# The first and second weight sums of a feed-forward chunk kept in other tiles

## The chip, the cores and the metric

The kernel runs on one core of a Trainium2 chip (trn2). The metric is the device time of one execution in microseconds. The profile is of one such execution; its times are counted from the start of its span.

## What is computed

Four layers of a transformer trunk on 256 tokens of width 1024, all in f32. Each layer is a feed-forward stage, an attention (differential, MoBA, NSA, differential) and a second feed-forward stage, each between two norms, so there are eight feed-forward stages:

```
def swiglu(x, w_in, w_out):
    gate, up = jnp.split(x @ w_in, 2, axis=-1)
    return (jax.nn.silu(gate) * up) @ w_out
...
h = h + 0.5 * rms_norm(swiglu(rms_norm(h, g[0]), ffn_w_in[i, 0], ffn_w_out[i, 0]), g[1])
```

`w_in` is 1024 x 5632, `w_out` 2816 x 1024. The attention is not touched by the change.

## The kernel before

**Splitting.** To keep f32 accuracy every operand of a matmul is split in two: ScalarE (ACT) rounds it to `hi` (line 156), VectorE (DVE) takes the rest, `lo = x - hi` (line 157). A product is then three matmuls (hi hi, lo hi, hi lo), at line 152 for the first products and lines 244 to 246 for the output product.

**Tiles.** Weights arrive as raw tiles of 128 x 2048 f32 (1 MB). A feed-forward stage has nine raw tiles, three in a pool of the whole program and six in a pool of the stage (`homes`). A split weight is a "unit", a hi and a lo tile; there are four units (the split ring). A unit comes free when the last matmul that reads it is done.

**Chunks.** The hidden width of 2816 is worked in six chunks, 512 columns each but for chunk 1 with 256. Chunks 0 and 1 are plain. Chunks 2 to 5 (`wino`, line 475) are multiplied by Winograd's form of the 2 x 2 block product (two token tiles; two halves of the inner dimension; gate and up), with seven products in place of eight. It needs sums of the quarters of the weights, b00 and b01 (upper half, gate and up), b10 and b11 (lower half): t1 = b00 + b01, t3 = b01 + b11, t2 = t1 + b11, t4 = t2 + b10. Matching signs are in the sums of the activations (lines 270 to 273).

Two of these sums are made by DVE (`add`, line 372) and two by an accumulating DMA that POOL issues (`add_by_dma`, line 375). Before the change t1 is made in b00 in place, t3 in b01 in place, t2 in a fifth raw tile, which is claimed without a load, and t4 there by DMA.

**Order.** `loads` and `preps` are two lists of steps, and `fill` (line 407) takes steps from them: loads while fewer than nine raw tiles are live, splits while fewer than four units are live. It is called behind each product. The preps of a wino chunk j, with the output weights ("o") of chunk j-1 among them, are written by `plan_wino` (line 359) in this order: split b00; split b10, then t1 and the DMA for t3; split o; t2, split t2, then the DMA for t4; splits of t1, t3, b11; the second o; the split of t4. TensorE's products of the chunk come in the order b00, b10, t2, t1, t3, b11, t4. Between them stand the transposes of the previous chunk's result (`turn`, line 439), which need its `g` (`up`, line 431), and its output products.

The program is written out in this order, and a scheduler of the framework then sets the order on each engine ahead of time. It lets an instruction pass others when its inputs are ready by its own estimate, and it gives a raw tile to whatever first writes to it. So the order in the trace is not always that of the source. At run time every engine and every DMA queue works in its fixed order; SP issues the loads (line 312).

Of the kernel before, what the change touches and what calls it, by code (L numbers as in the profile page):

```python
# [46 lines left out]
class Trunk:  # L47
# [235 lines left out]
    def ffn(self, l, f, X, ahead, end):  # L283
        nc = self.nc
        with self.tc.tile_pool(name=f"ffn{l}{f}", bufs=2, reuse_waits="tile") as pool:
# [8 lines left out]
            loads, preps = [], []  # L294

            def raw(n, src=None):
                live["raw"] += 1
                self.n += 1
                home = homes.pop(0)
                more = {} if home is self.raw else {"bufs": RAWS - 3}  # L300
                r = home.tile([P, 2048], F32, tag="raw", name=f"raw{self.n}", **more)
                R[n] = r
                H[n] = home
                if src is not None:
                    W, r0, nk, c0, w = src
                    v = r.rearrange("p (k n) -> p k n", n=w)[:, :nk] if nk * w == 2048 else \
                        r[:, :nk * w].rearrange("p (k n) -> p k n", n=w)
                    s = W[r0:r0 + nk * P, c0:c0 + w].rearrange("(k p) n -> p k n", p=P)
                    m = 1 if self.first_units > 0 else nk
                    self.first_units -= 1  # L310
                    for k in range(0, nk, m):
                        nc.sync.dma_start(v[:, k:k + m], s[:, k:k + m])
                    shape[n] = (nk, w, min(m, nk // 2) if n[0] == 0 and n[1] != "o" else nk)
                    if self.first_units == 2:
                        self.load_x(1)
# [3 lines left out]
            def free(n):  # L319
                R.pop(n)  # L320
                homes.append(H.pop(n))
                live["raw"] -= 1

            def split(n, of, done=False):
                live["unit"] += 1
                self.n += 1
                nk, w, m = shape.get(of, (4, 512, 4))
                hi = self.wt.tile([P, nk, w], F32R, tag="hi", name=f"hi{self.n}")
                lo = self.wt.tile([P, nk, w], F32R, tag="lo", name=f"lo{self.n}")
                v = R[of][:, :nk * w].rearrange("p (k n) -> p k n", n=w)  # L330
                for k in range(0, nk, m):
                    self.hilo(v[:, k:k + m], hi[:, k:k + m], lo[:, k:k + m])
                if done:
                    free(of)
                U[n] = hi, lo, nk, w
# [23 lines left out]
            def plan_wino(j):  # L359


                c0, w = chunks[j]
                name = lambda n: (j, n)
                quarter = lambda k, u: (w_in, k * 512, 4, u * D_FF + c0, w)
                c1, w1 = chunks[j - 1]
                ko = [((j - 1, "o", k), (w_out, c1 + k * P, 2, 0, D)) for k in range(0, w1 // P, 2)]
                for n, src in ((name("b00"), quarter(0, 0)), (name("b01"), quarter(0, 1)),
                               (name("b10"), quarter(1, 0)), (name("b11"), quarter(1, 1)), (name("t2"), None), *ko):
                    loads.append(lambda n=n, src=src: raw(n, src))

                def add(to, a, b):
                    nc.vector.tensor_tensor(R[name(to)], R[name(a)], R[name(b)], op=ALU.add)  # L372

                def add_by_dma(to, b):
                    nc.gpsimd.dma_start(R[name(to)], R[name(b)], accum_op=ALU.add)  # L375

                def quarters(n, then=()):
                    split(name(n), name(n))
                    for x in then:
                        (add if len(x) == 3 else add_by_dma)(*x)  # L380

                def last_of(n, of, gone=None):
                    split(name(n), name(of), True)
                    if gone:
                        free(name(gone))

                outs = [lambda n=n: split(n, n, True) for n, _ in ko]

                def split_t2():
                    add("t2", "b00", "b11")  # L390
                    quarters("t2", [("t2", "b10")])

                preps.extend([
                    lambda: quarters("b00"),
                    lambda: quarters("b10", [("b00", "b00", "b01"), ("b01", "b11")]),
                    outs[0],
                    split_t2,
                    lambda: last_of("t1", "b00"),
                    lambda: last_of("t3", "b01"),
                    lambda: last_of("b11", "b11")])  # L400
                if j < last:
                    preps.extend(outs[1:])
                preps.append(lambda: last_of("t4", "t2", "b10"))
                if j == last:
                    preps.extend(outs[1:])

# [123 lines left out]
            for j in range(1, last + 1):  # L530
                if j in WINO:
                    plan_wino(j)
                else:
                    plan_plain(j)
                    plan_out(j - 1)
# [795 lines left out]
```

## Time and profile before

| | us |
|---|---|
| median of 3 runs | 1992.58 (1991.72 to 1995.25) |
| the profiled execution | 1992.68 |
| its span, first to last instruction | 1991.0 |
| PE busy | 1934.5 |
| DVE busy | 1610.7 |
| ACT busy | 1261.7 |

The span is the time on the chip from the first to the last instruction, 1.7 us less than the execution's own time. Busy times are sums over all stages. Matmuls are pipelined, and each one's duration is longer than the step to the next, so PE's busy time doesn't show short gaps; the timeline does.

### The profile page before, as it was taken

To read this page: it belongs to the slowest core of one execution; us is meant where nothing else is said; L and a number is where in the kernel's file an instruction comes from. 1 tells how busy PE (TensorE), PEld (TensorE's weight loads), DVE (VectorE), ACT (ScalarE), POOL (GpSimd) and SP (SyncE) were. 2 spreads that over 40 slices of the span, in tenths; PEclk is the share of its full clock that TensorE was granted. 3 is DMA by queue.
4 is the path that set the end of the run, shared out by engine and by line. 5 is a ranking of instruction groups with operands and counts; after the bars stand their busy time and mean duration, and the time that the engine had idled before them with its cause. 6 is when DMAs were issued, how large, how long until landed. Compare 5 with 4: busy or idle time off the path is not lost.

```text
span 1991.0 us, 25740 instructions
## 1 busy us (share of the span) xinstructions
PE 1934.5 (97%) x9712; PEld 1582.6 (79%) x9712; DVE 1610.7 (81%) x2040; ACT 1261.7 (63%) x1721; POOL 187.2 (9%) x303
## 2 busy tenths in 40 slices
PE   7999999999999999999999998999999999999998
PEld 6788878788878878878887887678788788878787
DVE  6799678799789766789879977877998798678797
ACT  6566666566566666566656666865666567576564
POOL 0000210000000120000000032000000000210000
PEclk9999999999999999999999999999999999999999
DMA  9795638696787556587868775166879685638692
GB/s 359 215 281 161 211 118 314 162 283 209 258 238 236 182 191 212 189 246 232 291 199 244 210 205 165 58 242 191 238 214 322 177 285 161 202 106 306 176 289 64
DMA packets 177867, 430.25 MB, mean 216 GB/s; under 512 B 8784, under 2 KB 37712, under 8 KB 169552
## 3 DMA queue, kind: packets, MB, share of 16 engines
q1 hardware_dynamic: 168528, 361.51, 50.7%
q0 software_dynamic: 9216, 67.11, 18.1%
q8 instruction: 76, 1.25, 0.3%
q14 instruction: 47, 0.39, 0.1%
HBM read 360.43 MB, written 1.05 MB: 182 GB/s over the span
## 4 chain that ended last, share of the span: by engine, by line
PE 66%; DVE 11%; issue 10%; DMA 6%; ACT 4%; POOL 0%; POOLq 0%; DVEq 0%; ACTq 0%
PE pb L152 12%; PE ps L152 8%; PE y L244 7%; PE y L246 7%; PE y L245 7%; PE pc L152 6%; DVE lo L157 5%; PE pw L675 4%; DMA raw<-raw 4%; PE pw L677 4%; PE pw L676 3%; PE pa L152 3%; ACT hi L156 2%; DMA raw<-in_ffn_w_in 2%; DVE raw L372 2%
## 5 line engine op out<-in xcount | busy, mean ns | idle before, releaser
L157 DVE TENSOR_TENSOR lo<-raw,hi 128x2048 fp32r<-128x2048 f32 (+3 forms) x534 | 981.0, 1862 | 227.1 <-ACT hi L156 226.5
L156 ACT CAST hi<-raw 128x2048 fp32r<-128x2048 f32 (+3 forms) x534 | 818.9, 1560 | 327.0 <-PE y L246 168.9
L244 PE MATMUL y<-hi,gh 128*128 128x512 f32 x704 | 278.5, 396 | 0.0
L245 PE MATMUL y<-lo,gh 128*128 128x512 f32 x704 | 274.4, 390 | 0.0
L246 PE MATMUL y<-hi,gl 128*128 128x512 f32 x704 | 267.4, 393 | 0.0
L152 PE MATMUL ps<-hi,xh 128*128 128x256 f32 (+1 forms) x512 | 175.4, 343 | 1.9 <-ACT xh L156 1.3
L152 PE MATMUL ps<-lo,xh 128*128 128x256 f32 (+1 forms) x512 | 173.1, 338 | 0.2 <-DVE lo L157 0.2
L152 PE MATMUL ps<-hi,xl 128*128 128x256 f32 (+1 forms) x512 | 172.9, 338 | 0.0
L675 PE MATMUL pw<-hi,xh 128*128 128x512 f32 (+2 forms) x432 | 164.6, 381 | 0.0
L152 PE MATMUL pb<-lo,sh 128*128 128x512 f32 x384 | 153.4, 400 | 5.7 <-DVE lo L157 5.7
L677 PE MATMUL pw<-hi,xl 128*128 128x512 f32 (+2 forms) x432 | 155.7, 360 | 0.0
L676 PE MATMUL pw<-lo,xh 128*128 128x512 f32 (+2 forms) x432 | 155.4, 360 | 0.0
L375 POOL DMA_DIRECT2D raw<-raw x64 | 55.5, 868 | 1059.7 <-DVE raw L372 506.9
L246 PEld LDWEIGHTS y<-hi,gl 128*128 128x128 f32 x704 | 131.6, 188 | 29.1 <-DVE gl L157 1.5
L152 PE MATMUL pb<-hi,sh 128*128 128x512 f32 x384 | 153.5, 400 | 0.5
L244 PEld LDWEIGHTS y<-hi,gh 128*128 128x128 f32 x704 | 132.3, 188 | 27.1 <-ACT gh L156 1.2
L245 PEld LDWEIGHTS y<-lo,gh 128*128 128x128 f32 x704 | 132.4, 188 | 26.3
L152 PE MATMUL pb<-hi,sl 128*128 128x512 f32 x384 | 150.2, 391 | 0.0
L372 DVE TENSOR_TENSOR raw<-raw,raw 128x2048 f32<-128x2048 f32 x64 | 146.3, 2286 | 0.3
L152 PEld LDWEIGHTS ps<-hi,xh 128*128 128x128 f32 x512 | 97.6, 191 | 13.1 <-ACT xh L156 2.2
L152 PEld LDWEIGHTS ps<-lo,xh 128*128 128x128 f32 x512 | 97.7, 191 | 11.2 <-DVE lo L157 1.1
L152 PEld LDWEIGHTS ps<-hi,xl 128*128 128x128 f32 x512 | 97.4, 190 | 11.1 <-DVE xl L157 1.1
(213 smaller groups left out, 3301.4 us busy)
## 6 DMA issues: line engine op xcount, KB each, us to landing
raw<-in_ffn_w_in SPq DMA_DIRECT2D x172, 1024.0 KB, 8.9
raw<-in_ffn_w_out SPq DMA_DIRECT2D x88, 1024.0 KB, 9.7
raw<-raw POOLq DMA_DIRECT2D x64, 1024.0 KB, 8.1
raw<-in_diff_w_in SPq DMA_DIRECT2D x24, 1024.0 KB, 5.3
raw<-in_moba_w_in SPq DMA_DIRECT2D x12, 1024.0 KB, 5.1
raw<-in_nsa_w_in SPq DMA_DIRECT2D x9, 1024.0 KB, 5.1
raw<-in_diff_w_out SPq DMA_DIRECT2D x8, 1024.0 KB, 4.9
gpre<-in_norm_g SPq DMA_DIRECT2D x12, 512.0 KB, 6.3
```

The source lines that it names most:

```text
L152: nc.tensor.matmul(out, l, r, start=first and i == 0, stop=last and i == len(steps) - 1, skip_group_check=more)
L156: self.nc.scalar.copy(hi, src)
L157: self.nc.vector.tensor_tensor(lo, src, hi.bitcast(F32), op=ALU.subtract)
L244: nc.tensor.matmul(y[b], x[0][:, kt, :], hi[:, k, s], start=f, stop=False)
L245: nc.tensor.matmul(y[b], x[0][:, kt, :], lo[:, k, s], start=False, stop=False)
L246: nc.tensor.matmul(y[b], x[1][:, kt, :], hi[:, k, s], start=False, stop=l)
L372: nc.vector.tensor_tensor(R[name(to)], R[name(a)], R[name(b)], op=ALU.add)
L375: nc.gpsimd.dma_start(R[name(to)], R[name(b)], accum_op=ALU.add)
L675: nc.tensor.matmul(out, x[0][:, kt, :], hi[:, k, :], start=first and i == 0, stop=False)
L676: nc.tensor.matmul(out, x[0][:, kt, :], lo[:, k, :], start=False, stop=False)
L677: nc.tensor.matmul(out, x[1][:, kt, :], hi[:, k, :], start=False, stop=last and i == len(todo) - 1)
```

## The change

t1 gets the tile that was claimed without a load, and is written right behind the split of b00 (in the source, ahead of the split of b10), with the DMA for t3 behind it. t2 is then made in b00, whose own split is done, and t4 in b00 too, by DMA. b11 is loaded third and b10 last; before, b10 was third and b11 fourth.

```
-                for n, src in ((name("b00"), quarter(0, 0)), (name("b01"), quarter(0, 1)),
-                               (name("b10"), quarter(1, 0)), (name("b11"), quarter(1, 1)), (name("t2"), None), *ko):
+                for n, src in ((name("b00"), quarter(0, 0)), (name("b01"), quarter(0, 1)), (name("t1"), None),
+                               (name("b11"), quarter(1, 1)), (name("b10"), quarter(1, 0)), *ko):
...
-                def quarters(n, then=()):
-                    split(name(n), name(n))
-                    for x in then:
-                        (add if len(x) == 3 else add_by_dma)(*x)
-
-                def last_of(n, of, gone=None):
-                    split(name(n), name(of), True)
-                    if gone:
-                        free(name(gone))
+                def first():
+                    split(name("b00"), name("b00"))
+                    add("t1", "b00", "b01")
+                    add_by_dma("b01", "b11")
+
+                def second():
+                    add("b00", "t1", "b11")
+                    split(name("t2"), name("b00"))
+                    add_by_dma("b00", "b10")
+
+                def fourth():
+                    split(name("t4"), name("b00"), True)
+                    free(name("b10"))
...
-                def split_t2():
-                    add("t2", "b00", "b11")
-                    quarters("t2", [("t2", "b10")])
-
                 preps.extend([
-                    lambda: quarters("b00"),
-                    lambda: quarters("b10", [("b00", "b00", "b01"), ("b01", "b11")]),
+                    first,
+                    lambda: split(name("b10"), name("b10")),
                     outs[0],
-                    split_t2,
-                    lambda: last_of("t1", "b00"),
-                    lambda: last_of("t3", "b01"),
-                    lambda: last_of("b11", "b11")])
+                    second,
+                    lambda: split(name("t1"), name("t1"), True),
+                    lambda: split(name("t3"), name("b01"), True),
+                    lambda: split(name("b11"), name("b11"), True)])
                 if j < last:
                     preps.extend(outs[1:])
-                preps.append(lambda: last_of("t4", "t2", "b10"))
+                preps.append(fourth)
```

## Rows read from the trace of the kernel before

**Rows 1.** The page: busy time and share of the span of each engine

```profile
PE 1934.5 (97%) x9712; PEld 1582.6 (79%) x9712; DVE 1610.7 (81%) x2040; ACT 1261.7 (63%) x1721; POOL 187.2 (9%) x303
```

**Rows 2.** Waits of PE: who waited for whom, us in total, times, longest

```profile
PE tpg L439 <- DVE g L431: 20.8, 17, 1.3
...
PE pb L152 <- DVE lo L157: 5.7, 8, 0.7
```

**Rows 3.** Timeline of PE, first stage, chunk 3: start, us, instruction, [idle before]

```profile
90.82 0.33 PE L439 MATMUL tpg<-ident,g 128*128 128x128 f32 x1 [1.25 <-DVE g L431]
...
96.48 0.33 PE L439 MATMUL tpg<-ident,g 128*128 128x128 f32 x1 [1.33 <-DVE g L431]
...
100.13 0.50 PE L152 MATMUL pb<-lo,sh 128*128 128x512 f32 x1 [0.72 <-DVE lo L157]
```

**Rows 4.** Busy time by window: PE, PEld, DVE, ACT, POOL, PE clock, DMA

```profile
80.60:97.62 17.02, 14.44 (x65) 11.09 (x64) 17.02 (x12) 9.65 (x8) 0.84 (x1) 1.00 0.82 246
```

**Rows 5.** Timeline of DVE, first stage, the same stretch

```profile
80.60 2.29 DVE L157 TENSOR_TENSOR lo<-raw,hi 128x2048 fp32r<-128x2048 f32 x1 [2.87 <-ACT hi L156]
...
97.78 4.49 DVE L157 TENSOR_TENSOR lo<-raw,hi 128x2048 fp32r<-128x2048 f32 x2 [0.16 <-ACT hi L156]
```

**Rows 6.** Timeline of ACT, first stage, chunk 2

```profile
78.67 1.91 ACT L156 CAST hi<-raw 128x2048 fp32r<-128x2048 f32 x1 [3.26 <-DMA raw<-raw]
...
85.02 1.92 ACT L156 CAST hi<-raw 128x2048 fp32r<-128x2048 f32 x1 [0.36 <-DMA raw<-in_ffn_w_out]
```

**Rows 7.** Waits of ACT for the accumulating DMA, in all

```profile
ACT hi L156 <- DMA raw<-raw: 32.3, 10, 3.5
```

**Rows 8.** Timeline of ACT: the two of these that stand in chunk 5

```profile
650.98 1.91 ACT L156 CAST hi<-raw 128x2048 fp32r<-128x2048 f32 x1 [2.33 <-DMA raw<-raw]
...
1659.18 1.91 ACT L156 CAST hi<-raw 128x2048 fp32r<-128x2048 f32 x1 [2.66 <-DMA raw<-raw]
```

**Rows 9.** Timeline of PE, first stage: last reads of two units

```profile
61.08 0.39 PE L246 MATMUL y<-hi,gl 128*128 128x512 f32 x1
...
76.76 0.39 PE L246 MATMUL y<-hi,gl 128*128 128x512 f32 x1
```

**Rows 10.** Timeline of POOL: issue of the accumulating DMA for t4, chunks 2 and 3

```profile
70.40 0.86 POOL L375 DMA_DIRECT2D raw<-raw  x1 [16.53 <-DVE lo L157]
...
100.38 0.86 POOL L375 DMA_DIRECT2D raw<-raw  x1 [9.13 <-DVE lo L157]
```

**Rows 11.** Line 375, all 64 of them

```profile
DMA to landing us min/median/max: 6.9/8.1/10.6
```

**Rows 12.** Timeline of DVE, first stage, chunk 2

```profile
60.72 2.29 DVE L157 TENSOR_TENSOR lo<-raw,hi 128x2048 fp32r<-128x2048 f32 x1 [5.84 <-ACT hi L156]
63.05 2.29 DVE L372 TENSOR_TENSOR raw<-raw,raw 128x2048 f32<-128x2048 f32 x1
...
67.81 6.69 DVE L157 TENSOR_TENSOR lo<-raw,hi 128x2048 fp32r<-128x2048 f32 x3
```

**Rows 13.** Timeline of DVE, first stage, chunk 1: the first sum of chunk 2

```profile
49.96 2.29 DVE L372 TENSOR_TENSOR raw<-raw,raw 128x2048 f32<-128x2048 f32 x1
...
52.59 2.29 DVE L157 TENSOR_TENSOR lo<-raw,hi 128x2048 fp32r<-128x2048 f32 x1
```

**Rows 14.** Timeline of SP: loads of the weights

```profile
34.39 11.49 SPq L312 DMA_DIRECT2D raw<-in_ffn_w_in  x4
...
72.32 0.37 SPq L312 DMA_DIRECT2D raw<-in_ffn_w_in  x1
74.52 4.45 SPq L312 DMA_DIRECT2D raw<-in_ffn_w_out  x2
...
108.58 0.37 SPq L312 DMA_DIRECT2D raw<-in_ffn_w_in  x1
```

**Rows 15.** Timeline of DVE, chunk 3: the split of b11

```profile
105.44 2.29 DVE L157 TENSOR_TENSOR lo<-raw,hi 128x2048 fp32r<-128x2048 f32 x1 [0.35 <-ACT hi L156]
```

**Rows 16.** Timeline of PE, chunk 3: first read of lo of b11

```profile
111.31 0.39 PE L152 MATMUL pb<-lo,sh 128*128 128x512 f32 x1
```

## The prediction

> **What bounds the kernel now.** I read the page's busy times first: PE is busy for 1934.5 of 1991.0 us, 97% [rows 1]. So there is little to gain, and only where PE stands still. The waits of PE come next. Within the feed-forward stages two causes stand out [rows 2]: the transposes (line 439) wait for `g` from DVE, 20.8 us in 17 waits, and a product waits for `lo` from DVE, 5.7 us in 8. Eight is the number of feed-forward stages. The timeline of PE shows the place, the same in each stage, in the change from chunk 2 to chunk 3: waits of 1.25, 1.33 and 0.72 us at 90.82, 96.48 and 100.13 in the first stage [rows 3], 3.30 us per stage and 26.4 us in eight.
>
> What holds PE there is DVE's queue. From 80.60 to 97.62 DVE is busy for 17.02 of 17.02 us [rows 4], and PE only waits for what stands in that queue. The stretch begins with the lo of chunk 2's t4 at 80.60, for which DVE had idled 2.87 us, waiting for ACT's hi [rows 5]. That hi began at 78.67, behind 3.26 us of idle time that ended with the accumulating DMA [rows 6]. Two things are wanted by this split. One is a free unit: the last matmul on it ends at 76.76 + 0.39 = 77.15 [rows 9]. The other is the sum t4, whose DMA POOL issued at 70.40 [rows 10] and which arrived 8.27 us later; all 64 take 6.9 to 10.6 us, median 8.1 [rows 11]. The DMA came last. ACT had been free since 78.67 - 3.26 = 75.41, so the unit alone would have held it to about 77.20, 1.79 us of the 3.26.
>
> Why was the DMA issued at 70.40? It follows the lo of t2, the first of the three at 67.81 [rows 12], which follows the sum t2 at 63.05. That sum began right where the split of "o" of chunk 1 ended (60.72 + 2.29 = 63.01), though DVE had idled 5.84 us before that split [rows 12]. I read this as a wait for a raw tile: SP's four loads from 34.39 on [rows 14] had taken what was free, and t2's tile was the one that this split gave back.
>
> **The change, part by part.** Counts and sizes don't change: two DVE sums of 2.28 us and two accumulating DMAs per wino chunk, the same loads of 1 MB. What moves is when they can start.
>
> *The second sum, t2 into b00.* It needs no new tile, only t1, b11 and the finished split of b00. In chunk 2 it can go into DVE's 5.84 us of idle time before 60.72 (2.29 fit), and cover is found for it there at no cost. That the scheduler would take it forward is my inference from the first sum of chunk 2: it runs at 49.96, ahead of the lo of b10 at 52.59, behind which it is written [rows 13]. Then hi of t2 waits for its unit only, to 61.08 + 0.39 = 61.47 [rows 9], and ends at 61.5 + 1.9 = 63.4. Its lo follows to 65.7, and POOL can issue at 65.7 instead of 70.40. With 8.27 us the sum lands at 74.0, with the longest seen, 10.6, at 76.3. Both are before 77.15, so the wait for this DMA goes and the unit is late next. Worth: 3.26 - 1.79 = 1.47 us in the first stage.
>
> *Eight stages.* All waits of ACT for this DMA are 32.3 us in 10 [rows 7]; two stand in chunk 5, 2.33 and 2.66 [rows 8]; the other eight are 27.3. Less 8 x 1.79 = 14.3, this leaves **13.0 us**, 1.62 per stage. As DVE has no idle time from there to PE's last wait [rows 4], the whole queue moves forward by it, and PE's 3.30 us of waits shrink by the same.
>
> *The first sum, t1 into a tile of its own.* It needs no finished split of b00, but it needs a tile. For chunk 3 that comes from the stage's six, behind the loads of chunk 4's b00 and b01, which are written ahead of it; the third tile to come free there is that of chunk 2's t4, and the lo that frees it starts DVE's full stretch. So t1 stays in this stretch, as 2.28 us of the 17.02, only earlier in it. I take 0. Bounds: it leaves the stretch, -2.28 per stage, or it goes ahead of a step that PE waits for and PE loses all of it, +2.28 per stage.
>
> *The loads.* b10 of chunk 3 goes to the tile of chunk 2's t1, whose lo ended at about 72.3 before, where SP issued [rows 14], and should end near 69.5 now. The slowest landing seen here is that of the "o" load: issued at 74.52 [rows 14], waited for until 85.02 [rows 6], 10.5 us. b10 is then there at 80.0; ACT comes to it at about 81.5. Cost 0, up to 1 us per stage if the queue is fuller. SP has no step more in its queue, and in POOL's queue the DMAs stand where they stood or earlier.
>
> *Chunks 4 and 5.* In PE's timeline I found such waits only in the change to chunk 3, so nothing can be gained there. The costs are a rival's, below.
>
> **Sum.** 1992.68 (the profiled execution, 0.1 above the median) - 13.0 = **1979.7 us**. The mechanism's own range is 1973 to 1988: the DMA hidden better or worse by half.
>
> **Rivals.**
> *A. The first sum leaves the full stretch as well.* For: t1 asks for nothing but data that are there long before. Against: the tile. DVE's stretch would shrink by 1.62 + 2.28 = 3.9 us per stage, more than PE's 3.30 of waits, so 26.4 us go: 1966.3. Chance 0.13.
>
> *B. Nothing gained.* The second sum stays behind the split of "o" as it is written, at 63.05; then the DMA is issued at 70.40 again: 1992.7. Against: rows 13. The same time would come if the DMA were too short to be waited for. The trace says otherwise, with 8 of 8 stages waiting [rows 7] and a median of 8.1 us [rows 11]. The Trainium skill, "DMA: Bandwidth & Descriptors", section "Anatomy of one DMA", gives 2.0 us + bytes/436 GB/s for a DMA issued by POOL, 4.4 us for 1 MB as an estimate by that page: t4 would have landed at 74.8, the unit would be the later of the two, and the change would bring 0. Our 8.1 does not agree with it, perhaps because these DMAs add, and because loads run beside them. I give that rule 0.02 of the chance of 0.18 for B.
>
> *C. Slower: DVE's queue behind the DMA.* t1 of chunk 4 (and of 5) wants a free tile, and the next to come free may be the one that the accumulating DMA of the chunk before gives back. If the scheduler counts on an early landing, it puts the sum into the gap of 0.35 us before the lo of b11 at 105.44 [rows 15]. On the chip the DMA issued at 100.38 [rows 10] landed at 108.58, where SP's load takes its tile [rows 14]. The sum would end at 110.9 and the lo of b11 at 113.2. PE reads it at 111.31 [rows 16]: 1.8 us late. With the first gain moving all of this equally, the price stays. Once per stage it is 14.7 us and eats the gain: 1994.4. In chunks 4 and 5 both: 1979.7 + 2 x 14.7 = **2009**. It turns slower where more than 1.62 + 0.5 = 2.1 us per stage are lost. For: the tiles are short, and SP has waited for such a landing. Against: chunk 5's t1 has four loads ahead of it, so its tile likely comes from a split; and in chunk 2 SP's load at 74.52 [rows 14] waited for the lo of t3 and not for the DMA, so the scheduler doesn't expect this DMA to be very short. Chance 0.12.
>
> **How the numbers follow.** The forecast has 0.57, A 0.13, B 0.18, C 0.12. I predict 1979.7. The range must hold 8 in 10: forecast and B, and most of A's side: 1965 to 1995 leaves out C and a little of A. About 0.2% (4 us) is what a measurement here can tell from no change. Faster by more than that: forecast and A, 0.70. Within it: B, and C where it comes once, 0.19. Slower: 0.11.
>
> **What the profile will show.** Right: ACT's waits for the accumulating DMA fall from 32.3 us in 10 to the two of chunk 5; chunk 2's second sum stands before the split of "o"; POOL issues 4 to 5 us earlier; the lo of t4 starts 1.5 us earlier; PE's waits in chunk 3 fall from 3.30 to about 1.7 per stage, and PE's busy time is as before. A is seen if a sum of chunk 3 stands ahead of t4's lo, B if the sum is still at its old place. C is seen as DVE idling on an accumulating DMA or on a load in chunks 4 and 5. I would be wrong in kind if ACT's wait went and PE's waits stayed, or if new waits stood at the start of a stage, where the first sum may now be put among the norm's small steps.

## The result and the profile after

The changed kernel takes 1974.83 us, median of 4 runs (1973.12 to 1975.67), against 1992.87 us for the kernel before beside it: ratio 0.9907, 95% interval 0.989 to 0.9924. That is 18.0 us, where 13.0 were forecast. The profiled execution took 1973.12 us, with a span of 1971.1 us against 1991.0.

First the page: PE is as busy as in [rows 1], and the span is shorter. So PE stands still less.

```profile
PE 1929.6 (98%) x9712; PEld 1583.2 (80%) x9712; DVE 1610.2 (82%) x2040; ACT 1263.9 (64%) x1721; POOL 187.2 (9%) x303
```

The waits of PE (who waited for whom; us in total, times, longest) answer to [rows 2]. The transposes fall from 20.8 us to 2.8, while the products wait 16 times for `lo` in place of 8.

```profile
PE pb L152 <- DVE lo L157: 9.1, 16, 0.7
...
PE tpg L438 <- DVE g L430: 2.8, 7, 0.6
```

The timeline of DVE in the first stage (start, us, instruction, [idle before <- what ended it]) answers to [rows 5, 12, 13]. The trace after runs 0.36 us later up to here: the split of "o" stands at 61.08, before at 60.72.

```profile
44.75 2.28 DVE L372 TENSOR_TENSOR raw<-raw,raw 128x2048 f32<-128x2048 f32 x1
...
50.32 2.28 DVE L372 TENSOR_TENSOR raw<-raw,raw 128x2048 f32<-128x2048 f32 x1
...
61.08 2.29 DVE L157 TENSOR_TENSOR lo<-raw,hi 128x2048 fp32r<-128x2048 f32 x1 [5.84 <-ACT hi L156]
63.85 2.29 DVE L157 TENSOR_TENSOR lo<-raw,hi 128x2048 fp32r<-128x2048 f32 x1 [0.47 <-ACT hi L156]
...
76.22 4.53 DVE L157 TENSOR_TENSOR lo<-raw,hi 128x2048 fp32r<-128x2048 f32 x2 [3.10 <-ACT hi L156]
80.79 2.29 DVE L372 TENSOR_TENSOR raw<-raw,raw 128x2048 f32<-128x2048 f32 x1
```

Both sums of chunk 2 (44.75 and 50.32) are done ahead of the split of "o"; before, the second stood behind it, at 63.05. The lo of t2 follows at 63.85. The row at 76.22 is lo of b11 and of t4; the second starts near 78.5, before at 80.60. At 80.79 stands the first sum of chunk 3, still in the full stretch.

Then POOL's issue of t4's DMA, which was at 70.40 [rows 10], and ACT's hi of t4, which was at 78.67 behind 3.26 us of waiting for that DMA [rows 6].

```profile
66.45 0.86 POOL L375 DMA_DIRECT2D raw<-raw  x1 [17.79 <-DVE lo L157]
```

```profile
74.28 1.91 ACT L156 CAST hi<-raw 128x2048 fp32r<-128x2048 f32 x1
76.52 1.91 ACT L156 CAST hi<-raw 128x2048 fp32r<-128x2048 f32 x1 [0.33 <-PE y L246]
```

The DMA took 8.0 us and landed at 74.50. ACT waits for it no more; it waits 0.33 us for the unit. That unit is free at 76.09 + 0.39 = 76.48, not at the 77.15 + 0.36 = 77.51 of the forecast, because PE's order is another: the output product of the second token tile (lines 244 to 246) runs in one block of 12 matmuls. Before, half of t1's product stood inside it. PE's timeline shows the first and the last matmul of the block:

```profile
73.60 0.39 PE L244 MATMUL y<-hi,gh 128*128 128x512 f32 x1
...
76.09 0.39 PE L246 MATMUL y<-hi,gl 128*128 128x512 f32 x1
76.32 0.39 PE L152 MATMUL pb<-hi,sh 128*128 128x512 f32 x1
```

Where the 1.25, 1.33 and 0.72 us of [rows 3] stood, two shorter waits are left, both for a lo:

```profile
85.34 0.50 PE L152 MATMUL pb<-lo,xh 128*128 128x512 f32 x1 [0.47 <-DVE lo L157]
...
98.11 0.50 PE L152 MATMUL pb<-lo,sh 128*128 128x512 f32 x1 [0.65 <-DVE lo L157]
```

**The sum by place.** I laid the starts of the transposes of all chunks of both traces side by side. In the change to chunk 3 each stage becomes 2.3 to 2.9 us shorter, 21.9 us in eight. Behind that, mostly at the end of chunk 5, seven stages give back 0.1 to 0.8 us, 3.4 us in all. The NSA attention is 1.5 us shorter; in a second trace of the same changed kernel it is 1.6 us longer than before, so that part is scatter. With the 0.36 us at the start: 0.4 - 21.9 + 3.4 - 1.5 = -19.6, against 19.9 between the spans.

### The profile page after: what moved, and what is told of

The parts are those of the page before. It is cut to its first block, busy times and chain, and to the rows that moved or that the text cites. A ratio compares the mean times of both kernels' runs of the same rounds, so it can differ in the third digit from the quotient of the medians.

```text
span 1971.1 us, 25763 instructions
## 1 busy us (share of the span) xinstructions
PE 1929.6 (98%) x9712; PEld 1583.2 (80%) x9712; DVE 1610.2 (82%) x2040; ACT 1263.9 (64%) x1721; POOL 187.2 (9%) x303
## 3 DMA queue, kind: packets, MB, share of 16 engines
q8 instruction: 76, 1.25, 0.2%
HBM read 360.43 MB, written 1.05 MB: 183 GB/s over the span
## 4 chain that ended last, share of the span: by engine, by line
PE 64%; DVE 15%; issue 8%; ACT 6%; DMA 5%; POOL 1%; SPq 0%; DVEq 0%; POOLq 0%; ACTq 0%
PE ps L152 12%; DVE lo L157 9%; PE pb L152 9%; PE y L246 7%; PE y L244 7%; PE y L245 7%; ACT hi L156 4%; PE pw L674 4%; PE pw L676 4%; PE pw L675 4%; DMA raw<-raw 3%; PE pc L152 3%; DVE raw L372 2%; PE pa L152 2%; DMA raw<-in_ffn_w_in 1%
## 5 line engine op out<-in xcount | busy, mean ns | idle before, releaser
L152 PEld LDWEIGHTS ps<-lo,xh 128*128 128x128 f32 x512 | 97.7, 191 | 11.2 <-DVE lo L157 1.1
```

The costliest lines, as they stand in the source:

```text
L152: nc.tensor.matmul(out, l, r, start=first and i == 0, stop=last and i == len(steps) - 1, skip_group_check=more)
```

## Experiments

Each variant is told by its difference to the changed kernel, or to the kernel before where that is said.

**1. The tiles alone.** Loads in the old order, first sum behind the split of b10; only the tiles are as in the change.

```
-(name("b01"), quarter(0, 1)), (name("t1"), None),
-(name("b11"), quarter(1, 1)), (name("b10"), quarter(1, 0)), *ko):
+(name("b01"), quarter(0, 1)),
+(name("b10"), quarter(1, 0)), (name("b11"), quarter(1, 1)), (name("t1"), None), *ko):
...
 preps.extend([
-    first,
-    lambda: split(name("b10"), name("b10")),
+    lambda: split(name("b00"), name("b00")),
+    first,
```

In `first` the split is then that of b10, as shown in experiment 2.

> The changed kernel with two of its three parts undone: the loads are back in the old order (b10 third, b11 fourth, t1's tile fifth) and the first sum is back behind the split of b10. Only the tiles are as in the change: t1 in a tile of its own, t2 and t4 in b00. Theory: the gain is that the second sum waits for no free raw tile, so t4's DMA is issued 4 us earlier and ACT no longer waits for it. Then nearly all of the 18 us stays: 1977 us (1973 to 1982), and the second sum of chunk 2 stands near 50 us, POOL's issue near 66. Rival 1, the place of the first sum: without it the gain is gone, 1990 (1987 to 1993). Rival 2, the order of the loads (b11 there earlier): the same 1990.

Measured: 1978.66 us (1977.59 to 1980.91), ratio 0.9929 (0.9917 to 0.9942). Most of the gain is there, 13.5 of some 18 us, and the trace holds a control of its own. In the first stage the scheduler put the second sum at its old place, behind the split of "o" (first two rows); in the other seven it put it early (third row, second stage).

```profile
61.53 2.29 DVE L157 TENSOR_TENSOR lo<-raw,hi 128x2048 fp32r<-128x2048 f32 x1 [3.65 <-ACT hi L156]
63.74 2.29 DVE L372 TENSOR_TENSOR raw<-raw,raw 128x2048 f32<-128x2048 f32 x1
...
350.30 2.28 DVE L372 TENSOR_TENSOR raw<-raw,raw 128x2048 f32<-128x2048 f32 x1
```

ACT's hi of t4 in the same two stages:

```profile
79.49 1.91 ACT L156 CAST hi<-raw 128x2048 fp32r<-128x2048 f32 x1 [3.30 <-DMA raw<-raw]
...
376.46 1.91 ACT L156 CAST hi<-raw 128x2048 fp32r<-128x2048 f32 x1 [0.33 <-PE y L246]
```

The first stage gains nothing and keeps PE's old order, with t1's product inside the output product; the seven others gain 2.7 to 3.0 us in the change to chunk 3, and in all seven the block is there. So the gain goes with the early second sum, and PE's new order comes with both. This control doesn't part the DMA from PE's order; experiments 4 and 5 make the DMA late and keep the order.

**2. The first sum back behind the split of b10.** Loads and tiles as changed.

```
 def first():
-    split(name("b00"), name("b00"))
+    split(name("b10"), name("b10"))
     add("t1", "b00", "b01")
...
 preps.extend([
-    first,
-    lambda: split(name("b10"), name("b10")),
+    lambda: split(name("b00"), name("b00")),
+    first,
```

> The changed kernel with one part undone: the first sum and the DMA of t3 are written behind the split of b10 again; loads and tiles stay as changed. PE's order is that of the changed kernel. Theory: the place of the first sum is worth nothing, 1975 us (1972 to 1979); in chunk 3 the sum stands one lo later in DVE's stretch, and the waits of PE there change by less than 1 us per stage. Rival 1: 1990 (1987 to 1993). Rival 3, the sum ahead of t4's followers is a cost in the change (it stands in front of a lo that PE waits for, 9.1 us in 16 waits): then it gets faster, 1970 (1967 to 1973).

Measured: 1972.95 us (1972.58 to 1976.16), ratio 0.9902 (0.9889 to 0.9916). The written place is worth nothing that the times can show. In chunk 3 the scheduler puts the sum where it was (80.93, right behind the lo of t4); only in chunks 4 and 5 it moves, from 114.83 to 117.78 in the first stage. So rival 3 was not really tried: the sum stayed in front of the lo that PE waits for. Against experiment 1, which differs in the order of the loads alone, it is 5.7 us faster: 2.3 us of it in the first stage, and 1.7 us behind chunk 3, where t4's DMA of chunk 5 takes 8.1 us there and 7.8 here.

**3. The kernel before, with the loads and the first sum's place as changed.**

```
-(name("b10"), quarter(1, 0)), (name("b11"), quarter(1, 1)), (name("t2"), None), *ko):
+(name("b11"), quarter(1, 1)), (name("b10"), quarter(1, 0)), (name("t2"), None), *ko):
...
-lambda: quarters("b00"),
-lambda: quarters("b10", [("b00", "b00", "b01"), ("b01", "b11")]),
+lambda: quarters("b00", [("b00", "b00", "b01"), ("b01", "b11")]),
+lambda: quarters("b10"),
```

> The kernel before with the two other parts alone: b11 loaded third and b10 fourth, and the first sum (in b00 in place) with the DMA of t3 written right behind the split of b00. t2 and t4 keep the fifth tile. Theory: nothing, 1992.6 us (1989 to 1996): the second sum still waits for the tile that the split of o gives back, POOL issues near 70 and ACT waits 27 us for t4 in chunk 2. Rivals 1 and 2: 1975 to 1982, most of the gain without the tiles.

Measured: 1993.22 us (1991.68 to 1995.20, 11 runs), ratio 1.0001 (0.9992 to 1.001). Nothing. The second sum of the first stage stands at 63.54, behind the split of "o", and ACT waits 32.6 us for the accumulating DMA, as in [rows 7]. Without the tiles the other two parts are worth nothing; with them the order of the loads is worth some 5 us.

**4. POOL made late.** Six additions on POOL between the lo of t2 and the issue of t4's DMA, in chunk 2 alone. `self.late` is a new tile that nothing reads.

```
 split(name("t2"), name("b00"))
+if j == 2:
+    lo = U[name("t2")][1]
+    for i in range(6):
+        nc.gpsimd.tensor_tensor(self.late, R[name("b00")][:, :128], lo[:, 3, 384:].bitcast(F32), op=ALU.add)
 add_by_dma("b00", "b10")
```

> The changed kernel with POOL made late in chunk 2 alone: between the lo of t2 and the issue of t4's DMA POOL makes six small additions (128x128, into a tile that nothing reads), some 4 us. The order on PE, DVE, ACT and SP is that of the changed kernel. Theory: in the first stage the DMA is then issued near 70.5 in place of 66.45 and lands near 78.5, while the unit is free at 76.5. ACT's hi of t4 comes 2 us later in each stage, and PE, which waits for DVE's queue there, loses 8 x 2 = 16 us: 1991 (1986 to 1995). Rival 4: the DMA of t4 was not what the change gained by; the unit comes free earlier because PE's order changed (the output product of the second token tile runs in one block), and the rest follows from that order. Then a late DMA costs less than 0.5 us per stage: 1975 to 1979.

Measured: 2019.45 us (2017.58 to 2020.82), ratio 1.0132 (1.0118 to 1.0145): 44.6 us above the changed kernel, where 16 were expected. The additions took 1.2 us each, not 0.7, so the DMA goes out at 73.01 and ACT's hi of t4 comes at 80.69. POOL, then ACT, in the first stage:

```profile
65.57 7.13 POOL L389 TENSOR_TENSOR late<-raw,lo 128x128 f32<-128x128 f32 x6 [17.57 <-DVE lo L158]
73.01 0.88 POOL L376 DMA_DIRECT2D raw<-raw  x1 [0.31 <-POOL late L389]
```

```profile
80.69 1.90 ACT L157 CAST hi<-raw 128x2048 fp32r<-128x2048 f32 x1 [4.93 <-DMA raw<-raw]
82.50 0.58 ACT L514 COPY g<-pb 128x512 f32<-128x512 f32 x1
82.97 3.71 ACT L157 CAST hi<-raw 128x2048 fp32r<-128x2048 f32 x2
88.77 1.90 ACT L157 CAST hi<-raw 128x2048 fp32r<-128x2048 f32 x1 [2.08 <-DMA raw<-in_ffn_w_out]
```

Rival 4 (the DMA doesn't matter) falls. What the hi holds up is more than I had counted: ACT's copy of `g` is queued behind it, and PE waits for that copy (14.3 us in 8), and then for a lo of chunk 3 that stands behind t4's in DVE's queue (25.2 us in 9). A weight load of "o" comes late too (ACT waits for it 17.1 us in 8), but no wait of PE in that stretch ends with its split.

**5. Half of that.** Three additions.

```
-    for i in range(6):
+    for i in range(3):
```

> As the run with POOL made late, with three additions in place of six: 7.1 us of delay in the first stage there, so 3.5 us here. t4's DMA in chunk 2 is then issued at about 70.2 in the first stage, which is when the kernel before issued it, with PE's order as in the changed kernel. It lands near 78, the unit is free at 76.5, ACT's hi comes 1.5 us later. Theory: the loss is 1.5 to 1.9 us per stage, 12 to 15 us: 1987 us (1984 to 1990). That would be the share of the DMA in the gain of some 2.7 us per stage, and the rest (1 us) comes of PE's order, by which the unit is free 1 us earlier. Rival: the whole gain is the DMA's, then the time of before is back, 1992 to 1996.

Measured: 2009.76 us (2009.12 to 2010.22), ratio 1.0085 (1.007 to 1.01): neither expectation, worse than the kernel before. The first stage is again a control. There the additions took only 1.53 us, in the second stage 3.46:

```profile
66.39 1.53 POOL L389 TENSOR_TENSOR late<-raw,lo 128x128 f32<-128x128 f32 x3 [17.58 <-DVE lo L158]
68.23 0.88 POOL L376 DMA_DIRECT2D raw<-raw  x1 [0.31 <-POOL late L389]
...
363.92 3.46 POOL L389 TENSOR_TENSOR late<-raw,lo 128x128 f32<-128x128 f32 x3 [31.48 <-DVE lo L158]
367.73 0.87 POOL L376 DMA_DIRECT2D raw<-raw  x1 [0.36 <-POOL late L389]
```

ACT's hi of t4 in the same two stages:

```profile
76.91 1.91 ACT L157 CAST hi<-raw 128x2048 fp32r<-128x2048 f32 x1 [0.33 <-PE y L247]
...
378.09 1.90 ACT L157 CAST hi<-raw 128x2048 fp32r<-128x2048 f32 x1 [4.48 <-DMA raw<-raw]
```

Issued 1.6 us later than in the changed kernel, the DMA (8.1 us) costs next to nothing, 0.2 us of the stage: it is still there before the unit. Issued 3.5 us later it takes 10.1 to 11.2 us in all seven stages, so it lands later than before the change, though it went out earlier in the stage. The DMA queues during this one transfer (packets, MB, share of 16 engines) show 1.05 MB of weight loads beside it in the second stage of this run (first fence). In the changed kernel (second fence) it was 0.66 MB, in 8.0 us:

```profile
q0 software_dynamic: 144, 1.05, 49.1%
q1 hardware_dynamic: 528, 1.05, 37.6%
```

```profile
q0 software_dynamic: 144, 1.05, 75.4%
q1 hardware_dynamic: 337, 0.66, 23.0%
```

Part of the delay is repeated by SP, whose third load in the row waits for the landing. SP's queue in the second stage, first of the changed kernel, then of this one:

```profile
360.39 11.74 SPq L312 DMA_DIRECT2D raw<-in_ffn_w_in  x3
372.24 3.31 SPq L312 DMA_DIRECT2D raw<-in_ffn_w_out  x2
```

```profile
360.86 17.54 SPq L313 DMA_DIRECT2D raw<-in_ffn_w_in  x3
378.50 0.96 SPq L313 DMA_DIRECT2D raw<-in_ffn_w_out  x2
```

The DMA lands at 363.73 + 8.0 = 371.7 and at 367.73 + 10.3 = 378.0, and SP goes on 0.5 us later. I infer the wait from these times; the load of "o" behind it is late by as much.

**6. The control.** The six additions behind the issue of the DMA (they read lo of t2 alone).

> The control for the two runs with POOL made late: the same six additions on POOL in chunk 2, written behind the issue of t4's DMA in place of ahead of it. Theory: POOL has nothing else to do there, so they cost at most what they slow DVE's copies beside them (2.54 for 2.29 us, once per stage): 1975 to 1979 us. Rival: the additions themselves, not the late DMA, cost the time (DVE slowed beside them): over 1990.

Measured: 1974.70 us (1974.47 to 1975.81), ratio 0.991 (0.9896 to 0.9925). The additions themselves cost nothing; the late DMA does.

One number carries all these runs: the start of ACT's hi of t4, counted from the stage's first transposes in chunk 2. Beside it is the length from there to the first transposes in chunk 4 (us, least and most of the stages named):

| kernel | stages | hi of t4 | length |
|---|---|---|---|
| before | 1 to 8 | 14.6 to 14.9 | 60.6 to 60.9 |
| changed | 1 to 8 | 11.8 to 12.1 | 58.0 to 58.3 |
| tiles alone | 1 | 14.7 | 60.6 |
| tiles alone | 2 to 8 | 11.8 to 12.1 | 57.9 to 58.2 |
| three additions | 1 | 12.4 | 58.5 |
| three additions | 2 to 8 | 15.9 to 17.0 | 62.0 to 64.0 |
| six additions | 1 to 8 | 16.4 to 17.8 | 63.1 to 65.8 |
| control | 1 to 8 | 11.8 to 12.1 | 58.0 to 58.3 |

From changed to before the hi is on average 2.9 us later and the stretch 2.7 us longer, nearly one for one. Beyond that some stages are dearer, and what differs there is the clock that TensorE is granted. With three additions the second stage has its hi 4.5 us later than in the changed kernel, a stretch 4.5 us longer, and a clock of 1.00. The third has its hi 4.1 us later and a stretch 6.0 us longer, and behind PE's waits the clock falls. Busy time by window in these two stages, columns as in [rows 4]:

```profile
380.53:395.53 15.00, 11.87 (x53) 9.49 (x54) 14.97 (x10) 7.29 (x7) 0.85 (x1) 1.00 0.94 300
564.23:579.23 15.00, 11.91 (x41) 9.25 (x41) 13.97 (x9) 5.64 (x4) 0.86 (x1) 0.77 0.94 298
```

**7. The end of chunk 5.** In the changed kernel ACT has new waits for t4's DMA there, 2.75 to 2.96 us in seven stages. The DMA takes 7.7 to 7.9 us there; in the last stage, which has no next one, it takes 6.9 and ACT doesn't wait for it. ACT, first and last stage, then SP's loads for the next stage, which before began at 174.30:

```profile
168.76 1.91 ACT L156 CAST hi<-raw 128x2048 fp32r<-128x2048 f32 x1 [2.84 <-DMA raw<-raw]
...
1938.34 1.91 ACT L156 CAST hi<-raw 128x2048 fp32r<-128x2048 f32 x1 [2.24 <-PE y L246]
```

```profile
164.98 20.43 SPq L131 DMA_DIRECT2D raw<-in_diff_w_in  x4
```

The queues during t4's DMA of chunk 5 in the first stage show 0.25 MB of these loads beside it; in the last stage there is no load at all:

```profile
q0 software_dynamic: 144, 1.05, 74.6%
q1 hardware_dynamic: 121, 0.25, 8.8%
```

```profile
q0 software_dynamic: 144, 1.05, 74.8%
```

In the kernel before the same DMA took 7.2 us in the first stage, with no load beside it.

The variant splits the second "o" ahead of t4 in the last chunk too.

```
-if j < last:
-    preps.extend(outs[1:])
+preps.extend(outs[1:])
 preps.append(fourth)
-if j == last:
-    preps.extend(outs[1:])
```

> The changed kernel with one more step moved, in the last chunk alone: the split of the second output tile (o) stands ahead of the split of t4, as it does in the other chunks, so that the DMA of t4 has one product longer to land. In the changed kernel ACT waits 2.75 to 2.96 us for this DMA in 7 of 8 stages, and some 0.5 us per stage of the gain are given back there. Theory: that wait is what costs it, because the DMA takes 7.7 to 7.9 us beside the next stage's loads, which start earlier than before, against 6.9 in the last stage, which has none behind it. With the later split the wait goes: 1971 us (1968 to 1974), 0.5 us per stage faster. Rival: the unit would not have been free earlier anyway, or t4 is late for its product instead: 1974 to 1980.

Measured: 1973.44 us (1970.31 to 1973.92), ratio 0.9904 (0.9887 to 0.992). In its trace ACT's waits for this DMA are gone, and the eight stages give back nothing behind chunk 3 (0.0 us in sum), where the changed kernel gave 3.4. The time alone can't tell this from no change.

**8. The steps of experiments 2 and 7 together, and the changed kernel beside them.**

> The version with the last chunk's step moved, and the first sum behind the split of b10 as before. A candidate for the fastest. Theory: both are worth what they were alone, 0 to 2 us for the first sum and 3 to 4 for the last chunk: 1970 us (1966 to 1973). Rival: the place of the first sum was noise and the last chunk gains nothing: 1973 to 1977.

Measured: 1971.40 us (1970.50 to 1972.74), ratio 0.9893 (0.9878 to 0.9908). It was run again beside the changed kernel:

> The changed kernel itself, unaltered, on the same chip and beside the same runs of the kernel before as the candidate, since the candidate's difference to it (some 3 us) is below what runs of different chips can tell. Both theories: 1973 to 1976 us.

> The candidate again (first sum behind the split of b10; in the last chunk the second output tile split ahead of t4), beside the changed kernel. Theory: the last chunk's wait for t4's DMA was worth 0.4 to 0.5 us in 7 of 8 stages, so it is 2 to 4 us faster than the changed kernel: 1970 to 1972. Rival: no difference over 1 us.

Measured: the changed kernel 1974.22 us (1972.78 to 1975.30), ratio 0.9904 (0.989 to 0.9919); the candidate 1970.91 us (1969.29 to 1974.35), ratio 0.9893 (0.9876 to 0.9909). That is 3.3 us in this pair. The intervals overlap, but the medians of both of its runs are below those of the changed kernel, and the traces of this pair show 2.3 us of it behind chunk 3 (3.2 us given back in eight stages, 0.9 in the candidate). Its medians are the lowest here.

## Why the prediction was right, and where it was off

The sign, the place and the mechanism held; the size was too small.

**What bounds the kernel** held: DVE's queue behind the lo of t4. Experiments 4 and 5 lengthen the stage by making t4's DMA, and with it ACT's hi of t4, late. SP's next loads come late with it, but no wait of PE in that stretch ends with a split of them.

**The second sum** held as put: it went ahead of the split of "o" at 50.32, POOL issued 4 us earlier, and ACT's wait for this DMA is gone in chunk 2 (in the sixth stage, where it took 9.7 us, 0.4 us is left).

**The mis-sized term** is the unit's, "Less 8 x 1.79 = 14.3". I took the unit's time from the old order of PE, 77.15. With the second sum early the scheduler writes PE's output product in one block, and the unit is free at 76.48, 1.03 us earlier on that clock. Measured in the first stage, the hi moved from 78.67 + 0.36 = 79.03 to 76.52, by 2.5 us where 1.47 were forecast; 8 stages gave 21.9 us where 13.0 were forecast. All eight stages show it. Counted from the stage's first transposes in chunk 2, the unit is free at 13.1 us in each of them before, and at 12.1 in the first and 11.8 in the others after; the DMA lands at 14.6 to 14.8 before and 10.1 to 11.8 after. With the unit at 13.1 the hi would have come 1.6 us earlier per stage, the 13 us of the forecast; it came 2.9 us earlier. The scheduler sets the orders of DVE and PE together, so a term read from the old order of PE was no constant. Why the one order brings the other was not tried.

**A term that I left out** works the other way: chunk 5 gives 3.4 us back. I wrote that chunks 4 and 5 have nothing to gain, and priced a loss there only as rival C. The loss came otherwise: raw tiles come free earlier, so the next stage's loads begin at 164.98 in place of 174.30, run beside t4's DMA, and it takes 7.7 to 7.9 us against 6.9 in the last stage, where none runs, and 6.9 to 7.6 in all stages before, where none ran. Experiment 7 takes the wait away; that it is the loads which slow the DMA rests on the queues shown there, and was not tried by itself.

**The signs.** PE's waits in the change to chunk 3 fell from 3.30 to 1.12 us in the first stage, further than the 1.7 forecast. One sign came out otherwise: ACT's waits for the accumulating DMA fell from 32.3 us to 20.3 in 8, and not to the two of chunk 5; seven of the eight are those of experiment 7.

**The first sum** at 0 held: it stays in the stretch (80.79), and its written place is worth nothing. In chunk 2 of stages 2 to 8 it went to the start of the stage (328.39 in the second), among the small steps where the prediction feared new waits; the stretch up to chunk 2's first transposes did not get longer. **The loads** at 0 were not quite right: nothing alone, 5 us with the tiles, as experiments 1 to 3 show; why the scheduler keeps the second sum of the first stage late under the old order stays open. The slowest landing that the prediction named, 10.5 us, was not the slowest there: the load issued at 79.06 took 11.0. Nothing in the sum rests on it.

**The rivals.** A is not seen: the sum stands behind t4's lo. B is seen only in the first stage of experiment 1, and there with the price that I gave it, no gain. The Trainium skill's "DMA: Bandwidth & Descriptors", section "Anatomy of one DMA", would make this DMA 4.4 us as an estimate; no run agrees, with 6.9 to 12.3 us, and by 4.4 us experiment 5 would have cost nothing. Of the two reasons that the prediction gave for the difference, the loads beside it are not enough, for with none it took 6.9 us or more; whether the adding makes the rest, no run tests. C is not seen: the first sum of chunk 4 stands at 114.83, behind the lo of b11 at 103.45, and waits for no DMA.

## What to carry to other kernels

Where an accumulating DMA feeds a ring of few slots, look for what its issue waits for: here a sum waited for a free tile that it didn't need, and making it in place was worth 0.9%. When two waits end close together, don't price the second from the old schedule, for the schedule may move with the first. Then ask what the tiles that come free earlier will let start, and beside which transfer it runs.

## What the runs showed of the hardware

The accumulating DMA of 1 MB takes longer with more loads beside it, but their bytes alone do not set its time. Of the 768 in twelve traces, 75 had no load beside them and took 6.9 us in the median and 8.7 at most; 21 with 1.0 to 1.1 MB took 7.9 to 11.2, and 11 with over 2 MB took 11.5 to 12.3. With 1.05 MB it took 10.3 us in the second stage with three additions, and 8.7 in the third stage of the control; what makes that difference stays open. So a later issue can cost more than the delay, or less: three additions made it 3.5 us later at POOL and 4.0 to 6.7 us later at its landing, while with six, 7.2 us later at POOL, it took 7.0 us in six of eight stages, with at most 0.06 MB beside it.

A standstill of PE can cost a second time. With six additions, in the first stage, PE waits 1.64 and 3.13 us, and then the matmuls of `pc` step by 0.43 us where 0.23 is usual: the granted clock is 0.50 from 90.31 to 93.70, the lower of TensorE's two levels, 1.2 GHz. PE's timeline, and the busy time by window (PE, PEld, DVE, ACT, POOL, granted clock, DMA share, GB/s):

```profile
83.13 0.50 PE L153 MATMUL pb<-hi,sh 128*128 128x512 f32 x1 [1.64 <-ACT g L514]
...
89.50 0.50 PE L153 MATMUL pb<-lo,xh 128*128 128x512 f32 x1 [3.13 <-DVE lo L158]
...
90.31 0.63 PE L153 MATMUL pc<-hi,xh 128*128 128x512 f32 x1
90.74 0.63 PE L153 MATMUL pc<-lo,xh 128*128 128x512 f32 x1
```

```profile
89.50:95.00 5.50, 5.50 (x17) 4.38 (x18) 5.50 (x4) 1.17 (x1) 0.00 (x0) 0.69 1.02 232
95.00:105.00 10.00, 10.00 (x50) 8.27 (x49) 9.39 (x9) 8.19 (x8) 0.86 (x1) 1.00 0.38 119
```

In the changed kernel, with waits of 0.47 and 0.65 us, the clock stays at 1.00 through this stretch, and so it does in the kernel before, with 1.25, 1.33 and 0.72. Nor does it fall each time: with three additions it stayed at 1.00 in the second stage behind waits of 1.19 and 3.13 us, and fell in the third behind 1.14 and 3.09.

Small additions on POOL varied as well: 128x128 took 0.5 us each in the first stage and 1.15 us in the second of the same run (experiment 5). In the first stage DVE stood idle until 67.55, 1.16 of the 1.53 us; in the second a lo on DVE ran beside them from 364.48 and took 2.57 us in place of 2.29. That the two slow each other fits these rows, and was not tried by itself.
